# Adaptive scale and shift of the first two k tiles: half of the sum moved from VectorE to TensorE, with the weights as the stationary operand

## The chip, the cores and the metric

The kernel runs on one core of a Trainium2 chip. A core has a matrix engine (TensorE, PE in the rows), a vector engine (VectorE, DVE), a scalar engine (ScalarE, ACT), a general engine (GpSimd, POOL) and a queue that issues transfers (SyncE, SP). The metric is the time of one execution on the device in microseconds (us); several executions of a kernel are summed up by their median.

## What is computed

One layer of a streaming-encoder trunk on 512 tokens of width 2048. A conditioning vector c gives, by one matrix product, the scale, shift and gate of both sub-layers, and the modulated input goes into a token mixer and then an MLP:

```python
mod = c @ w_ada[l] + b_ada[l]
sh1, sc1, g1, sh2, sc2, g2 = [m[:, None, :] for m in jnp.split(mod, 6, axis=-1)]
h = x * (1.0 + sc1) + sh1
mix = token_mixer(h, w_in[l], ...)        # starts with proj = h @ w_in
x = layer_norm(ALPHA * x + g1 * mix, ln1_g[l], ln1_b[l])
h = x * (1.0 + sc2) + sh2
ff = jnp.square(jax.nn.relu(h @ w_ff1[l])) @ w_ff2[l]
x = layer_norm(ALPHA * x + g2 * ff, ln2_g[l], ln2_b[l])
```

Only the first line, for sc1 and sh1, and what waits for it at the very start, is touched by the change.

## The kernel before

Channels are cut into 16 **k tiles** of 128. No product with `w_in` over a k tile can begin before the scale and shift of that tile's 128 channels are known, so the kernel begins with `start_k(k, w)`, which prepares w tiles at once: first tile 0 alone, then tile 1 alone, then tiles 2 to 5, 6 to 9, 10 to 13, and 14 and 15.

`start_k` loads the columns of `w_ada` that belong to its tiles (256 columns for one tile, scale and shift, over 16 row blocks of 128) in pieces of 1 MB into the tile `raw`, of which there are four buffers. `ada_acc` (line 215) walks over the 16 row blocks on VectorE: each instruction multiplies one block by one column of c (`col("c", i)`, a value per partition) and adds it into `adaz`; the first is a multiply alone (line 67), the others multiply and add (line 63). For a single tile there are two sums, taken in turn (`ways=2`), so that an instruction doesn't depend on the one just ahead of it. What is left is the sum over the 128 partitions. That is done on TensorE (line 299): a 128x128 piece of `adaz` is the stationary operand and a column of ones the moving one, which gives one column of the bank `sc`. Such a matmul of full fp32 operands is carried out as two passes, each with its own weight load, so that 4 matmuls are 8 PE instructions in the trace.

Then follow on VectorE the bias (`mod`, line 301) and plus one (line 303), on ScalarE `hf` = x times scale plus shift (line 308), and `split` (line 120), which writes the high part of `hf` (ScalarE) and the low part (VectorE) into `acts`. Weights are split in the same way into `wh` (ScalarE) and `wl` (VectorE), the small ones of `wkw` into `kwh` and `kwl`. Every product is made of three matmuls, high by high, low by high, high by low: `mm3` (lines 196 to 198) with the weight stationary, `mm3n` (lines 208 to 210) with the activation stationary.

The loop over `KGROUPS` takes tiles 0 and 1 as its first group: for each of both tiles, 15 matmuls of `wA` and `wkw` (banks `sa`, `mm`, `sb`), then two blocks of `wqi` over both tiles (18 matmuls each, evacuated by ScalarE into `qi_n`), then two blocks of `wq` (24 each, evacuated into `q_t`). The order on each engine is set by a scheduler from the priorities in `PRIO`; each engine then runs its instructions strictly in that order. Transfers are all issued by SP, in order too, and an issue into a buffer waits until the buffer's last reader is done.

Of the kernel before, what the change touches and what calls it, by code (L numbers as in the profile page):

```python
# [51 lines left out]
def trunk_kernel(ctx, tc, A, out):  # L52
    nc = tc.nc
    V, S, G, T = nc.vector, nc.scalar, nc.gpsimd, nc.tensor

    def act(o, i, f=AF.Copy, **kw):
        S.activation(o, i, f, **kw)  # L57

    def tt(o, a, b, op):
        V.tensor_tensor(o, a, b, op=op)  # L60

    def stt(o, a, s, b, op0, op1):
        V.scalar_tensor_tensor(o, a, s, b, op0=op0, op1=op1)  # L63

    def ts(o, a, s1, s2, op0, op1=None):
        if op1 is None:
            V.tensor_scalar(o, a, s1, None, op0=op0)
        else:
            V.tensor_scalar(o, a, s1, s2, op0=op0, op1=op1)
# [11 lines left out]
    def prio(name):  # L81
        if name not in PRIO:
            name += str(stage_no[0])
        return tc.high_priority(offset=PRIO[name])

    def bank(n="mm"):
        if "two" in pools:
            return two_banks()[:, 0]
        return pools[n].tile([128, 512], F32, name=n)
# [9 lines left out]
    def col(n, i=0, w=1):  # L99
        o = COLS[n][0]  # L100
        return cols[:, o + i:o + i + w]
# [5 lines left out]
    ones = P.tile([128, 128], F32, name="ones")  # L107
# [12 lines left out]
    def split(h, l, src):  # L120
        act(h, src)
        tt(l, src, h.bitcast(F32), OP.subtract)

    def load(src, shape, pool=None, tag="raw", bufs=4, prio_="w_load"):
        r = (pool or rawp).tile(shape, F32, name=tag, bufs=bufs)
        with prio(prio_):
            nc.sync.dma_start(r, src)
        return r
# [86 lines left out]
    def ada_acc(srcs, n, brow=None, ways=1, pool=None):  # L215


        z = (pool or AZ[0]).tile([128, ways * n], F32, name="adaz", bufs=2 if pool else 1)
        if brow is not None:
            G.memset(z, 0.0)  # L220
            with prio("ada_bias"):
                nc.sync.dma_start(z[0:1, :], brow)
        i = 0
        for s in srcs:
            r = load(s, [128, s.shape[1], n], *ada_raw, prio_="ada_load")
            with prio("ada"):
                for j in range(s.shape[1]):
                    o = z[:, (i % ways) * n:(i % ways + 1) * n]
                    if i < ways and brow is None:
                        ts(o, r[:, j], col("c", i), None, OP.mult)  # L230
                    else:
                        stt(o, r[:, j], col("c", i), o, OP.mult, OP.add)
                    i += 1
            yield z
# [43 lines left out]
    FP = first.enter_context(tc.tile_pool(name="first", bufs=2, reuse_waits="tile"))  # L278
# [2 lines left out]

    def start_k(k, w):

        if w == 4:
            src = A["adaS4"][(k - 2) // 4]
        else:
            src = A["adaS2"][k // 14][:, :, 256 * (k % 2):256 * (k % 2 + w)]
        step = 8 // w
        ways = 2 if w == 1 else 1
        for i, z in enumerate(ada_acc([src[:, a:a + step] for a in range(0, 16, step)], 256 * w,  # L290
                                      ways=ways, pool=FP)):
            if i < 2 * w - 1:
                yield
        ps = bank("sc")
        mod = FP.tile([128, 2 * w], F32, name="mod")
        for j in range(2 * w):
            for a in range(ways):
                c0 = (a * 2 * w + j) * 128
                T.matmul(ps[:, j:j + 1], z[:, c0:c0 + 128], ones[:, 0:1], start=a == 0, stop=a == ways - 1)
        with prio("mod"):  # L300
            tt(mod, ps[:, 0:2 * w], col("bS", 2 * k, 2 * w), OP.add)
            sc_ = mod.rearrange("p (k two) -> p k two", two=2)[:, :, 0]
            ts(sc_, sc_, 1.0, None, OP.add)
            for j in range(w):
                xk = FP.tile([128, SEQ], F32, name="xk")
                nc.sync.dma_start(xk, A["xT"][k + j])
                hf = FP.tile([128, SEQ], F32, name="hf")
                act(hf, xk, AF.Identity, scale=mod[:, 2 * j:2 * j + 1], bias=mod[:, 2 * j + 1:2 * j + 2])
                split(acts[:, k + j, 0], acts[:, k + j, 1], hf)
        ready[0] = k + w  # L310
        yield

    def start_all():
        k = 0
        while k < KT:
            w = 1 if k < 2 else min(4, KT - k)
            yield from start_k(k, w)
            k += w
# [106 lines left out]
    with prio("index"):  # L425
# [19 lines left out]
        ps = bank("sa")  # L445
# [3 lines left out]
        for t in range(3):  # L449
# [10 lines left out]
            for hf in range(2):  # L460
                ps = bank("sa")
# [10 lines left out]
            for h in range(IH):  # L472
                ps = bank("sa")
                for i in range(2):
                    T.matmul(ps[:, 0:nk], qs[:, h // 2, h % 2], ks[:, i, 0:nk], start=i == 0, stop=i == 1)
                r = IX.tile([128, SEQ], F32, name="relu", bufs=2)
# [47 lines left out]
    def rms_rows(pool, acc, n_, b):  # L524

        ps = bank(b)
        for t in range(NT):
            T.matmul(ps[:, t:t + 1], acc[:, t * 128:(t + 1) * 128], ones[:, 0:1], start=True, stop=True)
        rs = pool.tile([128, NT], F32, name="st", bufs=4)
        act(rs, ps[:, 0:NT], AF.Sqrt, scale=1.0 / n_, bias=eps[:, 0:1])  # L530
        V.reciprocal(rs, rs)
        ps = bank(b)
        for t in range(NT):
            dg = pool.tile([128, 128], F32, name="dg", bufs=2)
            act(dg, ident, scale=rs[:, t:t + 1])
            T.matmul(ps[:, t * 128:(t + 1) * 128], ones, dg, start=True, stop=True)
        return ps

    def square_sum(pool, tiles, bufs=(2, 3)):
        acc = pool.tile([128, SEQ], F32, name="qh", bufs=bufs[0])  # L540
        act(acc, tiles[0], AF.Square)
        for y in tiles[1:]:
            sq = pool.tile([128, SEQ], F32, name="s", bufs=bufs[1])
            act(sq, y, AF.Square)
            tt(acc, acc, sq, OP.add)
        return acc
# [18 lines left out]
    def pv(i):  # L565
        return prm[:, i]
# [18 lines left out]
    with prio("ssm0"):  # L585
        lr, li = col("lr", 0, 16), col("li", 0, 16)
        dt, mag, ang, n, r, cs, sn, t0, t1, den, fr, fi, l4r, l4i = [pv(i) for i in range(14)]
# [64 lines left out]
        for j in range(1, 4):  # L652
            a = (hs[:, 0, :, j - 1:j], hs[:, 1, :, j - 1:j])
# [146 lines left out]
    with prio("glu"):  # L800
# [3 lines left out]
        for m in range(4):  # L804
            ps = bank("sb")
# [6 lines left out]
        ps = rms_rows(GL, square_sum(GL, [u_t[:, m] for m in range(4)], (1, 1)), 512, "sb")  # L812
# [121 lines left out]
    with prio("mixer"):  # L934
# [7 lines left out]
        ps = rms_rows(AT, square_sum(AT, [z_t[:, m] for m in range(4)]), 512, "sa")  # L942
# [76 lines left out]
    with prio("ln1"):  # L1019
        for t in range(NT):  # L1020
# [3 lines left out]
            for kq in range(4):  # L1024
                ps = bank(("sa", "sb")[kq % 2])
                for j in range(4):
                    k = 4 * kq + j
                    T.transpose(ps[:, j * 128:(j + 1) * 128], r1[:, t, k * 128:(k + 1) * 128], ident)
                hf = WO.tile([128, 4, 128], F32, name="hf2", bufs=3)
                for j in range(4):  # L1030
                    k = 4 * kq + j
# [46 lines left out]
    def ev_tile():  # L1078
        return ST.tile([128, 512], F32, name="ev", bufs=6)
# [52 lines left out]
    for i, j in QUARTERS:  # L1132
        r = ev_tile()
# [21 lines left out]
    with prio("tx"):  # L1155
        for c in range(2):
            kk = slice(4 * c, 4 * c + 4)

            def get(i, j):
                o = st_tile()  # L1160
                nc.sync.dma_start(o, hx_d[:, 8 * i + 4 * c:8 * i + 4 * c + 4, (lo_t, hi_t)[j]])
                return o
# [4 lines left out]
            a, b_ = get(0, 0), get(0, 1)  # L1167
# [236 lines left out]
    for e in range(NS):  # L1404
# [3 lines left out]
        if e == 0:  # L1408
# [3 lines left out]
            z = []  # L1412
# [91 lines left out]
    for t in range(NT):  # L1504
        for i in range(2):
            ps = bank()
# [102 lines left out]
```

## Time and profile before

| | us |
|---|---|
| median of 3 runs | 2272.72 |
| the runs | 2266.93 to 2273.12 |
| the profiled execution, its own time | 2262.95 |
| its span on the core | 2261.2 |
| PE busy | 2159.0 (95%) |
| DVE busy | 1873.2 (83%) |
| ACT busy | 1092.9 (48%) |

The profile lists the busy time of each engine, the span in slices, the chain of work that ended last, and the trace gives every instruction with its start, its duration and what its engine waited for. Durations of matmuls overlap, since they are pipelined: the time that one takes of a stream is the distance from its start to the start of the next.

### The profile page before, as it was taken

To read this page: it belongs to the slowest core of one execution; us is meant where nothing else is said; L and a number is where in the kernel's file an instruction comes from. 1 tells how busy PE (TensorE), PEld (TensorE's weight loads), DVE (VectorE), ACT (ScalarE), POOL (GpSimd) and SP (SyncE) were. 2 spreads that over 40 slices of the span, in tenths; PEclk is the share of its full clock that TensorE was granted. 3 is DMA by queue.
4 is the path that set the end of the run, shared out by engine and by line. 5 is a ranking of instruction groups with operands and counts; after the bars stand their busy time and mean duration, and the time that the engine had idled before them with its cause. 6 is when DMAs were issued, how large, how long until landed. Compare 5 with 4: busy or idle time off the path is not lost.

```text
span 2261.2 us, 30621 instructions
## 1 busy us (share of the span) xinstructions
PE 2159.0 (95%) x11947; PEld 1849.2 (82%) x11947; DVE 1873.2 (83%) x2520; ACT 1092.9 (48%) x1570; POOL 44.6 (2%) x55
## 2 busy tenths in 40 slices
PE   6999999988899999999999999999999999999997
PEld 4778887866676787899999999999888887878886
DVE  7886889998776776798778778778699989998788
ACT  3323434458855223666555555555444444444432
POOL 0000000000000000000000000000000000000000
PEclk9999999999999999999999999999999999999999
DMA  8877553264224576745654544553788988796562
GB/s 320 320 292 278 182 216 135 96 208 154 79 84 172 208 282 264 242 142 205 212 187 178 199 183 176 197 187 140 289 303 281 335 276 290 236 343 226 146 235 90
DMA packets 129626, 485.59 MB, mean 215 GB/s; under 512 B 15556, under 2 KB 38468, under 8 KB 88264
## 3 DMA queue, kind: packets, MB, share of 16 engines
q1 hardware_dynamic: 122952, 471.04, 56.9%
q0 software_dynamic: 6528, 12.58, 3.3%
q8 instruction: 94, 1.54, 0.3%
q14 instruction: 52, 0.43, 0.1%
HBM read 392.35 MB, written 78.64 MB: 208 GB/s over the span
## 4 chain that ended last, share of the span: by engine, by line
PE 44%; DVE 32%; DMA 15%; ACT 5%; issue 4%; DVEq 0%; SPq 0%; ACTq 0%
DMA raw<-in_wff_dram 11%; DVE wl L60 10%; PE two L1375 4%; PE two L1376 4%; PE two L1374 4%; DVE st L60 4%; PE mm L210 4%; PE mm L209 4%; PE mm L208 4%; PE mm L197 4%; PE mm L198 4%; PE mm L196 4%; DVE ffa L60 2%; DVE adaz L63 2%; DVE hc L60 2%
## 5 line engine op out<-in xcount | busy, mean ns | idle before, releaser
L57 ACT ACTIVATE wh<-raw 128x1024 fp32r<-128x1024 f32 x332 | 349.5, 1057 | 427.4 <-PE two L1376 137.9
L60 DVE TENSOR_TENSOR wl<-raw,wh 128x1024 fp32r<-128x1024 f32 x332 | 403.1, 1220 | 69.4 <-ACT wh L57 68.9
L1375 PE MATMUL two<-wl,hin 128*128 128x512 f32 x784 | 307.8, 393 | 3.3 <-DVE wl L60 3.0
L1374 PE MATMUL two<-wh,hin 128*128 128x512 f32 x784 | 307.1, 392 | 3.8 <-ACT wh L57 2.1
L1376 PE MATMUL two<-wh,hin 128*128 128x512 f32 x784 | 306.1, 390 | 0.0
L196 PE MATMUL mm<-acts,wh 128*128 128x512 f32 (+1 forms) x568 | 225.5, 400 | 7.3 <-ACT ve L57 3.8
L203 PE MATMUL mm<-acts,wl 128*128 128x256 f32 x720 | 209.4, 291 | 18.4 <-DVE wl L60 18.2
L197 PE MATMUL mm<-acts,wl 128*128 128x512 f32 (+1 forms) x568 | 223.6, 394 | 1.9 <-DVE wl L60 1.7
L198 PE MATMUL mm<-acts,wh 128*128 128x512 f32 (+1 forms) x568 | 223.6, 395 | 0.0
L63 DVE SCALAR_TENSOR_TENSOR adaz<-raw,cols,adaz 128x1024 f32<-128x1024 f32 (+2 forms) x180 | 198.3, 1112 | 17.5 <-DMA raw<-in_adaR_dram 13.4
L202 PE MATMUL mm<-acts,wh 128*128 128x256 f32 x720 | 206.1, 286 | 1.3 <-ACT ev L57 1.3
L204 PE MATMUL mm<-acts,wh 128*128 128x256 f32 x720 | 206.0, 286 | 0.0
L203 PE MATMUL mm<-tx,wl 128*128 128x256 f32 x720 | 203.8, 283 | 0.0
L204 PE MATMUL mm<-tx,wh 128*128 128x256 f32 x720 | 203.3, 282 | 0.0
L202 PE MATMUL mm<-tx,wh 128*128 128x256 f32 x720 | 201.9, 280 | 0.0
L1375 PEld LDWEIGHTS two<-wl,hin 128*128 128x128 f32 x784 | 147.6, 188 | 40.3 <-DVE wl L60 9.2
L1374 PEld LDWEIGHTS two<-wh,hin 128*128 128x128 f32 x784 | 147.5, 188 | 36.0 <-ACT wh L57 3.0
L209 PE MATMUL mm<-wl,acts 128*128 128x512 f32 x448 | 175.0, 391 | 1.2 <-DVE wl L60 1.0
L210 PE MATMUL mm<-wh,acts 128*128 128x512 f32 x448 | 174.7, 390 | 0.0
L208 PE MATMUL mm<-wh,acts 128*128 128x512 f32 x448 | 173.6, 391 | 0.2 <-DVE r L60 0.2
L1376 PEld LDWEIGHTS two<-wh,hin 128*128 128x128 f32 x784 | 147.6, 188 | 30.4
L203 PEld LDWEIGHTS mm<-acts,wl 128*128 128x128 f32 x720 | 140.6, 195 | 24.4 <-DVE wl L60 24.4
(316 smaller groups left out, 4539.1 us busy)
## 6 DMA issues: line engine op xcount, KB each, us to landing
raw<-in_wff_dram SPq DMA_DIRECT2D x128, 1024.0 KB, 6.4
hc_d<-hc SPq DMA_DIRECT2D x98, 512.0 KB, 3.8
hin<-hc_d SPq DMA_DIRECT2D x49, 1024.0 KB, 9.0
raw<-in_adaR_dram SPq DMA_DIRECT2D x48, 1024.0 KB, 5.1
raw<-in_adaS_dram SPq DMA_DIRECT2D x32, 1024.0 KB, 9.0
raw<-in_wo_dram SPq DMA_DIRECT2D x16, 1024.0 KB, 5.0
araw<-in_adaR_dram SPq DMA_DIRECT2D x16, 1024.0 KB, 6.3
raw<-in_wconv_dram SPq DMA_DIRECT2D x12, 1024.0 KB, 4.8
```

The costliest lines, as they stand in the source:

```text
L57: S.activation(o, i, f, **kw)
L60: V.tensor_tensor(o, a, b, op=op)
L196: T.matmul(ps, wh, xh, start=start, stop=False)
L197: T.matmul(ps, wl, xh, start=False, stop=False)
L198: T.matmul(ps, wh, xl, start=False, stop=stop)
L202: T.matmul(ps, wh, xh, start=start, stop=False, skip_group_check=True)
L203: T.matmul(ps, wl, xh, start=False, stop=False, skip_group_check=True)
L204: T.matmul(ps, wh, xl, start=False, stop=stop, skip_group_check=True)
L209: T.matmul(ps, xh, wl, start=False, stop=False)
L1374: T.matmul(ps[:, t], xh, h[:, k], start=first, stop=False, skip_group_check=True)
L1375: T.matmul(ps[:, t], xh, l[:, k], start=False, stop=False, skip_group_check=True)
L1376: T.matmul(ps[:, t], xl, h[:, k], start=False, stop=last, skip_group_check=True)
```

## The change

For tiles 0 and 1 alone (`w == 1`), VectorE sums only the first 8 of the 16 row blocks, in one sum instead of two. The other 8 blocks are not summed on VectorE at all: each 128x128 piece of the loaded weights is the stationary operand of a TensorE matmul and the column of c that belongs to it the moving one (16 matmuls, line 294 of the changed kernel), all accumulating into the bank `sc`. The two pieces of `adaz` are added to the same bank with the column of ones (2 matmuls, line 297). The tiles prepared four and two at a time are summed as they were.

```diff
-        step = 8 // w
-        ways = 2 if w == 1 else 1
-        for i, z in enumerate(ada_acc([src[:, a:a + step] for a in range(0, 16, step)], 256 * w,
-                                      ways=ways, pool=FP)):
-            if i < 2 * w - 1:
-                yield
         ps = bank("sc")
         mod = FP.tile([128, 2 * w], F32, name="mod")
-        for j in range(2 * w):
-            for a in range(ways):
-                c0 = (a * 2 * w + j) * 128
-                T.matmul(ps[:, j:j + 1], z[:, c0:c0 + 128], ones[:, 0:1], start=a == 0, stop=a == ways - 1)
+        if w == 1:
+
+            src = A["adaS2"][k // 14][:, :, 256 * (k % 2):256 * (k % 2 + 1)]
+            for z in ada_acc([src[:, 0:8]], 256, pool=FP):
+                yield
+            r = load(src[:, 8:16], [128, 8, 256], prio_="ada_load")
+            for i in range(8):
+                for j in range(2):
+                    T.matmul(ps[:, j:j + 1], r[:, i, 128 * j:128 * j + 128], col("c", 8 + i),
+                             start=(i, j) == (0, 0), stop=False, skip_group_check=True)
+            for j in range(2):
+                T.matmul(ps[:, j:j + 1], z[:, j * 128:(j + 1) * 128], ones[:, 0:1], start=False, stop=True,
+                         skip_group_check=True)
+        else:
...
+            for j in range(2 * w):
+                T.matmul(ps[:, j:j + 1], z[:, j * 128:(j + 1) * 128], ones[:, 0:1], start=True, stop=True)
```

The order of all engines changes within about the first 60 matmuls and is the same behind them; SP issues its transfers in the same order as before. Three places:

TensorE, from the last matmul of tile 0 (bank `sb`) to the first ones of tile 1 (bank `sa`); `sc` is the bank of the scale and shift. Before:

```order
L198 MATMUL sb<-acts,kwh 80x512
L299 MATMUL sc<-ones,adaz 128x1 x4
L208 MATMUL mm<-wh,acts 128x512 x2
L209 MATMUL mm<-wl,acts 128x512
L210 MATMUL mm<-wh,acts 128x512
L196 MATMUL sa<-acts,wh 128x512
```

In the changed kernel, the same place:

```order
L198 MATMUL sb<-acts,kwh 80x512
L294 MATMUL sc<-cols,raw 128x1 x16
L297 MATMUL sc<-ones,adaz 128x1 x2
L196 MATMUL sa<-acts,wh 128x512
L197 MATMUL sa<-acts,wl 128x512
```

Four matmuls on `adaz` became 16 on the raw weights and 2 on `adaz`, and the four matmuls of `wqi` that stood between them and tile 1 moved behind tile 1. For tile 0 it is the same 16 and 2, at the head of the engine's program.

ScalarE, from tile 1's preparation to the evacuations of the first `wqi` block; the rows `wh<-rw 128x1024` split the weights of the first and of the second `wqi` block. The difference:

```order
-L57 ACTIVATE wh<-rw 128x1024
 L57 ACTIVATE hf<-xk,mod 128x512
 L57 ACTIVATE acts<-hf 128x512
+L57 ACTIVATE wh<-rw 128x1024
 L57 ACTIVATE u_t<-mm 128x512 x2
-L57 ACTIVATE wh<-rw 128x1024
 L57 ACTIVATE qi_n_105<-mm 128x512
 L57 ACTIVATE qi_n_106<-mm 128x512
 L57 ACTIVATE qi_n_107<-mm 128x512
+L57 ACTIVATE wh<-rw 128x1024
```

The split for the first block moved behind tile 1's `hf`, and the split for the second block moved from ahead of the first block's three evacuations to behind them.

VectorE, the head of its program in the changed kernel; before, 16 rows of `adaz` and then `wl` and `kwl` stood ahead of `mod`:

```order
L67 TENSOR_SCALAR adaz<-raw,cols 128x256
L63 SCALAR_TENSOR_TENSOR adaz<-raw,cols,adaz 128x256 x7
L60 TENSOR_TENSOR mod<-sc,cols 128x2
L67 TENSOR_SCALAR mod<-mod 128x1
L60 TENSOR_TENSOR wl<-rw,wh 128x512
L60 TENSOR_TENSOR kwl<-rkw,kwh 128x80
L60 TENSOR_TENSOR acts<-hf,acts 128x512
```

Eight rows of `adaz` are gone, and `wl` and `kwl` of tile 0 moved behind `mod`, which waits for TensorE's bank `sc`.

## Rows read from the trace of the kernel before

**Rows 1.** Page, the chain that ended last: share of the span by engine.

```profile
PE 44%; DVE 32%; DMA 15%; ACT 5%; issue 4%; DVEq 0%; SPq 0%; ACTq 0%
```

**Rows 2.** Windows of 10 us: length, busy us, granted clock, DMA share, GB/s.

```profile
10.00:20.00 10.00, 5.24 (x16) 4.42 (x17) 9.09 (x25) 3.03 (x6) 0.00 (x0) 1.00 1.09 370
20.00:30.00 10.00, 8.54 (x40) 6.37 (x39) 8.55 (x15) 4.64 (x6) 0.00 (x0) 1.00 1.01 413
```

**Rows 3.** Chain of waits, 5 to 16 us: start, us, what.

```profile
7.43 5.24 DVE adaz L63 x13
...
12.81 1.85 PE sc L299 x8
```

**Rows 4.** VectorE's timeline around the second transfer's landing: start, us, instruction.

```profile
9.33 0.48 DVE L63 SCALAR_TENSOR_TENSOR adaz<-raw,cols,adaz 128x256 f32<-128x256 f32 x1
9.81 0.48 DVE L63 SCALAR_TENSOR_TENSOR adaz<-raw,cols,adaz 128x256 f32<-128x256 f32 x1
```

**Rows 5.** Line 299 in two windows: duration min/median/max ns, first and last start.

```profile
L299 PE MATMUL sc<-ones,adaz x8: 345/352/352, 12.8 to 14.3; 128*128 128x1 f32 x8
L299 PE MATMUL sc<-ones,adaz x16: 164/250/250, 53.2 to 54.8; 128*128 128x1 f32 x16
```

**Rows 6.** TensorE's timeline, tiles 0 and 1: start, us, instruction, idle before it.

```profile
16.60 0.79 PE L196 MATMUL sa<-acts,wh 128*128 128x512 f32 x1 [1.95 <-ACT acts L57]
...
18.90 0.63 PE L197 MATMUL mm<-acts,wl 128*128 128x512 f32 x1
19.33 0.60 PE L196 MATMUL mm<-acts,wh 128*128 128x512 f32 x1
19.75 0.41 PE L197 MATMUL mm<-acts,wl 128*128 128x512 f32 x1
...
21.38 0.39 PE L198 MATMUL sb<-acts,kwh 128*80 128x512 f32 x1
22.21 1.13 PE L299 MATMUL sc<-ones,adaz 128*128 128x1 f32 x8 [0.44 <-DVE adaz L63]
```

**Rows 7.** TensorE's timeline, a later place with single-column matmuls (line 254).

```profile
300.13 0.39 PE L475 MATMUL sa<-ks,qs 128*128 128x256 f32 x1 [0.53 <-ACT relu L57]
300.36 0.28 PE L254 MATMUL sc<-ones,adaz 128*128 128x1 f32 x2
...
303.28 0.63 PE L196 MATMUL mm<-acts,wh 128*128 128x512 f32 x1
303.71 0.63 PE L197 MATMUL mm<-acts,wl 128*128 128x512 f32 x1
```

**Rows 8.** Chain of waits, 24 to 62 us, around the first `wq` blocks.

```profile
36.15 0.24 PE mm L210
...
36.41 0.60 ACT qi_n L57
37.01 0.95 ACT wh L57
37.98 1.24 DVE wl L60
...
39.27 0.50 PE mm L197
...
46.98 0.74 PE mm L197
...
50.66 0.23 PE mm L196
```

**Rows 9.** SP's timeline; VectorE's first instruction on the next tiles' weights.

```profile
12.92 0.92 SPq L127 DMA_DIRECT2D raw<-in_adaS_dram  x2
...
25.88 0.75 DVE L67 TENSOR_SCALAR adaz<-raw,cols 128x1024 f32<-128x1024 f32 x1
```

**Rows 10.** Chain of waits, 140 to 160 us: a load of the third set of tiles.

```profile
148.05 0.33 SPq L306
...
148.47 7.68 DMA raw<-in_adaS_dram
```

More of the change, by code (lines that the diff above doesn't have):

```diff
@@ L282, in start_k @@
     def start_k(k, w):
[L284 to L287, printed above, removed]
-        step = 8 // w
-        ways = 2 if w == 1 else 1
-        for i, z in enumerate(ada_acc([src[:, a:a + step] for a in range(0, 16, step)], 256 * w,
-                                      ways=ways, pool=FP)):
-            if i < 2 * w - 1:
-                yield
         ps = bank("sc")
         mod = FP.tile([128, 2 * w], F32, name="mod")
-        for j in range(2 * w):
-            for a in range(ways):
-                c0 = (a * 2 * w + j) * 128
-                T.matmul(ps[:, j:j + 1], z[:, c0:c0 + 128], ones[:, 0:1], start=a == 0, stop=a == ways - 1)
+        if w == 1:
[11 more added lines that the diff above has]
+        else:
+            if w == 4:
+                src = A["adaS4"][(k - 2) // 4]
+            else:
+                src = A["adaS2"][k // 14][:, :, 256 * (k % 2):256 * (k % 2 + w)]
+            step = 8 // w
+            for i, z in enumerate(ada_acc([src[:, a:a + step] for a in range(0, 16, step)], 256 * w, pool=FP)):
+                if i < 2 * w - 1:
+                    yield
+            for j in range(2 * w):
+                T.matmul(ps[:, j:j + 1], z[:, j * 128:(j + 1) * 128], ones[:, 0:1], start=True, stop=True)
         with prio("mod"):
```

## Prediction

> **What bounds the kernel now.** I read the chain that ended last by engine first: TensorE 44%, VectorE 32%, transfers 15% [rows 1]. The reader is to see that no one engine sets the whole time; stages pass the end to each other, so a change is worth what it does in its own stage. The change touches the first 36 us only; from the end of the second `wqi` block on, the order of all engines is as before. There I read the windows [rows 2]: VectorE is busy 9.1 of 10 us and 8.6 of 10 us while TensorE is at 5.2 and 8.5, which makes VectorE look like the place to save. The chain of waits says what stands behind that [rows 3]: 13 sums on `adaz` (5.24 us, 0.403 us each), then the column sums on TensorE, 12.81 to 14.66 us, then `mod`, `hf`, the high part, and at 16.60 the first product [rows 6]. So for tile 0 the sums are on the path. What the trace doesn't say directly is when the second half of the weights lands: at 9.33 to 9.81 two sums are 0.48 us apart where the others keep 0.40 [rows 4], and 9.81 is the ninth sum, the first on the second transfer. I take 9.8 us as its landing.
>
> The price of a TensorE pass is in two rows [rows 5]: 8 passes start from 12.8 to 14.3 us, about 0.212 us apart; 16 passes from 53.2 to 54.8, 0.106 apart. That is the two levels of the clock: the 512-column products of tile 0 are 0.43 us apart up to 19.75 us (1.2 GHz) and 0.23 after it (2.4 GHz) [rows 6], although the window view prints a granted clock of 1.00 there [rows 2]; I go by the spacings.
>
> **Tile 0.** Removed: 8 of 16 sums on VectorE, 4 of 8 passes. Added: 16 matmuls, that is 32 passes, which need the second half, so they can't begin before 9.8 us. TensorE has done nothing until then and runs at its lower level. Before, from 9.8 to the end of the column sums: 14.66 - 9.8 = 4.9 us. After: 36 passes x 0.212 = 7.6 us. VectorE's eight sums now depend on each other; the seven behind the first start at 7.43 [rows 3], and even at twice 0.403 us they'd end by 7.4 + 5.6 = 13.0 us, while the 32 passes run to 16.6, so they are hidden and cost nothing, and what VectorE saves is worth nothing. **+2.8 us.** Bounds: at 0.106 all through, 3.8 us, -1.1; at the lower level only for the 3.1 us that tile 0's products needed (16.60 to 19.75, [rows 6]), 14.6 passes, then 21.4 x 0.106: 5.4 us, +0.5. `wl` and `kwl` of tile 0 now queue behind `mod` on VectorE; a `wl` of twice the size takes 1.24 us [rows 8], and ScalarE needs 1.95 us from the column sums to the first product [rows 6], so they are done by then. The low part is next on VectorE and, at half of 1.24 us, ready 0.6 us after the first product starts, before the third one needs it at 0.43 us each: no loss.
>
> **Tile 1.** Before, from the end of tile 0's column sums to the end of tile 1's: 23.34 - 14.66 = 8.7 us [rows 3, 6]; VectorE's sums ended it. After, TensorE ends it, since its passes stand behind tile 0's 15 products: 1.95 us + 5.0 us (16.60 to 21.6, the same start at the lower level) + 36 passes. Those start at the higher level. But a later place has such passes too [rows 7]: from 300.36 us on TensorE is given 16 of them between four products of 256 columns, and behind them the 512-column products go from 0.23 us apart to 0.43 at about 303. So I let the clock fall 2.7 us after they begin: 25 passes at 0.106, 11 at 0.212, 5.0 us. In all 12.0: **+3.3 us**. Bounds: all at the higher level, 3.8 us, +2.1; all at the lower, 7.6 us, +5.9.
>
> **Tile 1's products and the two `wqi` blocks.** Before, 23.34 to 36.39: 13.05 us, with a wait for `wl` in it. After: 1.95 us, then 15 + 18 products x 0.23 = 7.6 us without a wait. Then comes a new one: the second block's `wh` now stands behind the three evacuations on ScalarE, and its `wl` on VectorE behind that. The trace has the same pattern one block later [rows 8]: from the block's end at 36.39, 0.60 us of `qi_n`, 0.95 of `wh`, 1.24 of `wl`, first low product at 39.27, so 2.88 us, of which 3 products fill 0.7. Then 15 x 0.23 = 3.4 us. In all 15.85: +2.8 us. After the passes and 1.95 us of waiting I expect the lower level for 3.1 us again: 7 products x 0.2 = 1.4 us. **+4.2 us.** Bounds: +2.8 if the clock stays; one more fall across the new wait costs 8 x 0.2 = 1.6 us as from 46.98 to 50.66 [rows 8], so +5.8.
>
> **Transfers.** Two loads for tiles 2 to 5 now wait until TensorE, not VectorE, has read a buffer. The first pair was issued at 12.92 us and is first used at 25.88 [rows 9]; it would now be issued at about 17 and used some 8 us later than before, since tile 1 is later. Cost nothing; if that cover were gone, the 4 us of the issue. Queued behind them on SP are the loads of `wqi` and `wq`, used more than 20 us later.
>
> **Sum.** 2.8 + 3.3 + 4.2 = +10.3 us; with each part's bounds around the likeliest mechanism, 2.8 + 2.1 + 2.8 = 7.7 to 2.8 + 5.9 + 5.8 = 14.5. After that the shift is carried on: each stage starts from the one before. Against the profiled execution that is 2262.95 + 10.3 = 2273.3. That execution lies 9.8 us below the median of the runs shown, and a measurement gives a median: 2272.7 + 10.3 = 2283.0, own range 2280 to 2287.
>
> **Rivals.** (1) **The passes raise the clock like products do.** Then tile 0 costs +0.5; tile 1 is 1.95 + 15 x 0.23 + 0.2 for the low part + 3.8 = 9.4, +0.7; the rest +2.8: +4.0, 2276.7. For it: the engine is busy in both. Against it: the fall behind such passes [rows 7]. The Trainium skill, TensorE: Matmul & The Clock Gate, Part 1: The HAM clock gate, says that the lower level is the default and that activity releases it, whatever the number of matmuls; by that page the sum would be this rival's +4.0. The rows at 300 us lean against counting these passes so.
>
> (2) **The delay is taken up later.** At 148.47 the chain waits 7.68 us for a load of the third set of tiles [rows 10]. Had that load been issued in time whatever came ahead, it would swallow up to 7.7 us: 2275.3. Against it: the issue stands on SP behind line 306, which ends at 148.4 only because `hf` was late, so it shifts too.
>
> (3) **VectorE sets the pace**, not the path through TensorE, and the change pays: 16 sums x 0.403 = -6.4 us, 2266.3. For it: VectorE's 9.1 and 8.6 of 10 us [rows 2]. It decides from the point where 36 passes fit into the 4.9 us of tile 0, at 0.135 us a pass. Against it: 0.212 at that very place [rows 5].
>
> (4) **More falls of the clock** in later short waits, each 1.6 us [rows 8]; three beyond the sum give +15.1, 2287.8. For it: two waits of about 2 us follow one another now. Against it: the sum already has one fall, behind the passes, and the products of one burst warm the clock for the next.
>
> **Chances.** A measurement of this kernel tells about 0.3% (6.8 us) from no change. Forecast 0.58, nearly all of it slower by more than that; rival 1 0.18, rival 2 0.09, both within; rival 3 0.07, mostly within, since 6.4 is below the bound; rival 4 0.08. Slower: 0.54 + 0.08 = 0.62; same: 0.04 + 0.18 + 0.09 + 0.04 = 0.35; faster 0.03. The range goes down to rivals 1 and 2 and up to rival 4: 2275 to 2288; left out are rival 3 and the far ends.
>
> **What would show it.** Line 294 starts near 9.8 us with passes 0.21 apart, and the first 512-column product near 19.3 us instead of 16.6; tile 1's passes slow down part of the way; tile 1's products start 0.43 apart; TensorE idles about 2 us between the `wqi` blocks; line 299's successor for tiles 2 to 5 comes some 10 us later than 53.2. Wrong if: passes on raw weights are below 0.14 us at the start, the second transfer lands clearly before 9.8, or the shift at 55 us is gone by 160.

## The result and the profile after

The changed kernel takes 2282.61 us, median of six runs (2280.71 to 2283.45), against 2272.06 us for the kernel before on the same chip (six runs, 2266.93 to 2273.12). The ratio is 1.0051, 95% interval 1.0038 to 1.0064: slower by about 11 us. The profiled execution took 2282.96 us and has a span of 2281.2 us.

The page of the changed kernel, busy time by engine and the chain that ended last, answers to the table of before and to [rows 1]:

```profile
PE 2175.4 (95%) x12003; PEld 1864.1 (82%) x12003; DVE 1867.3 (82%) x2504; ACT 1093.2 (48%) x1570; POOL 44.6 (2%) x55
...
PE 40%; DVE 35%; DMA 16%; ACT 5%; issue 4%; DVEq 0%; SPq 0%; ACTq 0%
```

The page hardly shows the change: VectorE did 16 instructions and 6 us less, TensorE 56 more. The shares of the chain move by up to four points, but they also differ between two executions of the changed kernel (TensorE 40% and 42%, VectorE 35% and 32%), so little can be read from them. The windows of 10 us do show the change (columns as in [rows 2]):

```profile
10.00:20.00 10.00, 8.05 (x37) 7.96 (x38) 2.28 (x7) 2.63 (x5) 0.00 (x0) 1.00 1.09 368
...
30.00:40.00 10.00, 8.06 (x24) 6.30 (x25) 6.75 (x8) 3.58 (x5) 0.00 (x0) 0.58 0.64 224
```

The last of these windows in the kernel before:

```profile
30.00:40.00 10.00, 8.32 (x36) 6.26 (x35) 8.79 (x8) 4.54 (x8) 0.00 (x0) 1.00 1.03 413
```

Between 10 and 20 us VectorE is busy 2.3 us where it was 9.1 [rows 2], so the change relieved the engine that looked full, and TensorE is busy 8 us where it was 5.2. Between 30 and 40 us the granted clock is 0.58 where it was 1.00. TensorE's timeline of the changed kernel (start, us, engine, line, instruction, idle before it and what ended it) answers to [rows 6]:

```profile
9.90 6.96 PE L294 MATMUL sc<-cols,raw 128*128 128x1 f32 x32 [9.90 <-DMA raw<-in_adaS_dram]
16.72 0.99 PE L297 MATMUL sc<-ones,adaz 128*128 128x1 f32 x4
19.66 0.79 PE L196 MATMUL sa<-acts,wh 128*128 128x512 f32 x1 [1.95 <-ACT acts L57]
...
24.52 0.48 PE L198 MATMUL mm<-acts,wh 128*128 128x512 f32 x1
...
25.52 4.46 PE L294 MATMUL sc<-cols,raw 128*128 128x1 f32 x32
29.84 0.99 PE L297 MATMUL sc<-ones,adaz 128*128 128x1 f32 x4
32.77 0.79 PE L196 MATMUL sa<-acts,wh 128*128 128x512 f32 x1 [1.94 <-ACT acts L57]
...
38.06 0.53 PE L196 MATMUL sb<-acts,kwh 128*80 128x512 f32 x1
38.43 0.40 PE L197 MATMUL sb<-acts,kwl 128*80 128x512 f32 x1
...
38.90 0.40 PE L208 MATMUL mm<-wh,acts 128*128 128x512 f32 x1
...
44.81 0.98 PE L208 MATMUL mm<-wh,acts 128*128 128x512 f32 x3 [1.63 <-ACT wh L57]
...
51.39 1.20 PE L196 MATMUL mm<-acts,wh 128*128 128x512 f32 x4 [1.63 <-ACT wh L57]
```

The 32 passes on raw weights start with the second transfer and the four on `adaz` start at 16.72, so a pass takes (16.72 - 9.90) / 32 = 0.213 us. The column sums end at 17.71 instead of 14.66, the first product starts at 19.66 instead of 16.60 [rows 6]. Tile 1's passes stand behind the last product of tile 0 without a gap and take 5.3 us. Tile 1's products are 0.43 us apart up to 38.06. The first `wqi` block starts at 38.90, ahead of 44.81 there is the new wait between the two blocks, and the first `wq` product starts at 51.39.

What VectorE did, from its own timeline in the changed kernel:

```profile
7.26 3.61 DVE L63 SCALAR_TENSOR_TENSOR adaz<-raw,cols,adaz 128x256 f32<-128x256 f32 x7
17.75 0.16 DVE L60 TENSOR_TENSOR mod<-sc,cols 128x2 f32<-128x2 f32 x1 [6.88 <-PE sc L297]
...
30.86 0.16 DVE L60 TENSOR_TENSOR mod<-sc,cols 128x2 f32<-128x2 f32 x1 [5.87 <-PE sc L297]
...
34.84 0.75 DVE L67 TENSOR_SCALAR adaz<-raw,cols 128x1024 f32<-128x1024 f32 x1
```

Its share of the sum is done at 10.87 us. Then it sits idle for 6.88 us, and later for 5.87 us, until TensorE has the bank `sc`: before, TensorE waited for VectorE at these places [rows 3, 6].

### The profile page after: what moved, and what is told of

The parts are those of the page before. It is cut to its first block, busy times and chain, and to the rows that moved or that the text cites. A ratio compares the mean times of both kernels' runs of the same rounds, so it can differ in the third digit from the quotient of the medians.

```text
span 2281.2 us, 30717 instructions
## 1 busy us (share of the span) xinstructions
PE 2175.4 (95%) x12003; PEld 1864.1 (82%) x12003; DVE 1867.3 (82%) x2504; ACT 1093.2 (48%) x1570; POOL 44.6 (2%) x55
## 4 chain that ended last, share of the span: by engine, by line
PE 40%; DVE 35%; DMA 16%; ACT 5%; issue 4%; DVEq 0%; SPq 0%; ACTq 0%
DVE wl L60 11%; DMA raw<-in_wff_dram 10%; PE two L1385 4%; PE two L1386 4%; PE two L1384 4%; DVE st L60 4%; PE mm L197 3%; PE mm L198 3%; PE mm L196 3%; PE mm L210 3%; PE mm L209 3%; PE mm L208 3%; DVE ffa L60 3%; DVE adaz L63 2%; DVE hc L60 2%
## 5 line engine op out<-in xcount | busy, mean ns | idle before, releaser
L63 DVE SCALAR_TENSOR_TENSOR adaz<-raw,cols,adaz 128x1024 f32<-128x1024 f32 (+2 forms) x166 | 193.3, 1165 | 16.8 <-DMA raw<-in_adaR_dram 13.8
L203 PEld LDWEIGHTS mm<-acts,wl 128*128 128x128 f32 x720 | 139.2, 193 | 24.5 <-DVE wl L60 24.2
```

Source lines behind the costliest of these rows:

```text
L203: T.matmul(ps, wl, xh, start=False, stop=False, skip_group_check=True)
```

## The experiments

All are read at the same four places: the end of tile 0's and of tile 1's column sums, the first product of the first `wq` block, and the first column sum of the third set of four tiles, each as its distance from the first profile of the kernel before (14.66, 23.34, 38.01 and 143.75 us), beside the ratio of the times to the kernel before on the same chip. The last column is the interval minus one, times 2271 us. The distances come from one execution each, and the two of the change lie 1.9 us apart at the first `wq`, so differences of that size between rows tell little.

| kernel | tile 0 | tile 1 | first `wq` | third set | ratio [95%] | in us |
|---|---|---|---|---|---|---|
| before, again | 0.0 | 0.0 | 0.0 | +0.2 | 1.0007 [0.9985, 1.0029] | -3 to +7 |
| the change | +3.1 | +7.5 | +13.4 | +13.6 | 1.0051 [1.0038, 1.0064] | +9 to +15 |
| the change, again | +2.9 | +5.5 | +11.5 | +11.9 | 1.0044 [1.0028, 1.0060] | +6 to +14 |
| tile 0 only | +2.8 | +4.5 | +7.1 | +7.2 | 1.0027 [1.0009, 1.0045] | +2 to +10 |
| tile 1 only | -0.1 | +4.3 | +10.1 | +10.0 | 1.0057 [1.0035, 1.0079] | +8 to +18 |
| fillers ahead | +1.6 | +3.8 | +9.7 | +10.0 | 1.0067 [1.0047, 1.0087] | +11 to +20 |
| split ahead | +2.8 | +7.3 | +10.4 | +9.9 | 1.0034 [1.0021, 1.0047] | +5 to +11 |
| a quarter on TensorE | -0.2 | +1.6 | +1.7 | +0.8 | 1.0003 [0.9988, 1.0019] | -3 to +4 |
| before, filled | +0.4 | +1.0 | +2.8 | +2.9 | 1.0013 [0.9990, 1.0036] | -2 to +8 |

**The kernel before, again.** No edit. The first profile of the kernel before was 9 us below its median, and the profile of the changed kernel lies 20 us above it, twice what the medians differ by. The question was which part of that belongs to the change.

> The kernel before, once more, for a second profile. In the two profiles so far the changed kernel is 13.4 us late at the end of the second wqi block (49.77 against 36.39 us) and 12.4 us late at 70 us, and stays so up to 300 us; between 300 and 710 us it falls back by 7.5 us more, to 20 in span, while the medians differ by 10.5. Theory (the loss is made in the first 60 us, the 7.5 us are where the clock of TensorE happens to fall in an execution): this profile ends the second wqi block at 36.4 us again, within 0.5 us, is within 1 us of the first profile up to 300 us, and then falls behind it by 5 to 10 us, to a time near 2272. Rival (the later 7.5 us belong to the change): it stays within 2 us of the first profile to the end, near 2263.

It follows the first profile within about 0.2 us up to the third set and within 0.8 us at line 254 (first start 299.62 against 300.36 [rows 7]), and ends 8.6 us later (span 2269.8 against 2261.2). The window from 300 to 710 us of the first profile of the kernel before, and under it of this second one (columns as in [rows 2]; the granted clock is the third number from the end):

```profile
300.00:710.00 410.00, 377.32 (x1727) 289.61 (x1728) 349.78 (x852) 239.87 (x516) 11.90 (x19) 0.98 0.41 144
```

```profile
300.00:710.00 410.00, 376.49 (x1706) 291.08 (x1705) 343.88 (x844) 236.82 (x509) 11.91 (x19) 0.95 0.41 143
```

The same program had a granted clock of 0.98 there once and 0.95 once, and between the first pass of line 254 at 300 us and its last one ahead of 700 us (661.0 and 665.7) the second execution falls behind by 5.4 us. So the clock behind 300 us differs from one execution to the next whatever the change, and the first profile was a lucky one. From 300 us on the profiles can't be set against each other one by one; up to 300 us they can.

**The change for tile 0 only.** Tile 1 is summed as before, in two sums on VectorE.

```diff
-        if w == 1:
+        if w == 1 and k == 0:
...
+        elif w == 1:
+            src = A["adaS2"][k // 14][:, :, 256 * (k % 2):256 * (k % 2 + 1)]
+            for i, z in enumerate(ada_acc([src[:, a:a + 8] for a in range(0, 16, 8)], 256, ways=2, pool=FP)):
+                if i < 1:
+                    yield
...
```

> The change for tile 0 alone; tile 1 is summed on VectorE as before. Theory (the passes run at the lower level of the clock on the path, and tile 1's part and the moved order cost apart from it): column sums of tile 0 end at 17.7 us against 14.66, +3.1; second wqi block ends at 39.5 to 41 us against 36.39 of before and 49.77 of the changed kernel; no new wait between the wqi blocks, since the order of ScalarE there is that of before; time 3 to 4 us above before, near 2275.5. Rival (the loss is made in the later part, or by the buffers that come free later): as late as the changed kernel, 2282.

Tile 0 costs what it costs in the changed kernel, +2.8 us. But 7.1 us were lost at the first `wq` block, about twice what was expected. TensorE's timeline of this kernel behind tile 0's products:

```profile
26.67 1.13 PE L307 MATMUL sc<-ones,adaz 128*128 128x1 f32 x8 [1.00 <-DVE adaz L63]
...
29.98 0.63 PE L196 MATMUL sa<-acts,wh 128*128 128x512 f32 x1
30.41 0.63 PE L197 MATMUL sa<-acts,wl 128*128 128x512 f32 x1
```

Tile 1's sums, now started later on VectorE, end later (+4.5 us), and tile 1's products come at the lower level, 0.43 us apart, where before they stood 0.23 apart (25.51 to 28.72 us). So here the delay at the head is followed by a second loss, in the clock.

**The change for tile 1 only**, by the same edit with `k == 1`.

> The change for tile 1 alone; tile 0 is summed on VectorE as before. Theory: column sums of tile 0 end at 14.7 us; tile 1's passes begin at 21.6, where its products end, and end at 25.5 to 27.1 against 23.34; tile 1's products run at the lower level for at least 3 us; 2.2 us of TensorE idle between the wqi blocks, since ScalarE's order there is that of the changed kernel; second wqi block ends at 43 to 46 us; time 6.5 to 9 us above before, 2278.5 to 2281. Rival (tile 0 alone makes the loss and the rest follows from it): less than 2 us above before.

Ten us at the first `wq` block, more than was expected. Its timeline on TensorE:

```profile
21.95 4.87 PE L294 MATMUL sc<-cols,raw 128*128 128x1 f32 x32
26.68 0.99 PE L297 MATMUL sc<-ones,adaz 128*128 128x1 f32 x4
30.26 0.80 PE L196 MATMUL sa<-acts,wh 128*128 128x512 f32 x1 [2.59 <-ACT acts L57]
...
41.56 0.98 PE L208 MATMUL mm<-wh,acts 128*128 128x512 f32 x3 [1.63 <-ACT wh L57]
```

Although tile 0 is done as before, 36 passes take 5.7 us here; all at the higher level would be 36 x 0.106 = 3.8 [rows 5]. The wait between the `wqi` blocks is the same as in the whole change, so it belongs to the order that comes with tile 1. The parts don't add up (7.1 + 10.1 against 13.4). Tile 1's own steps in the table are those of the whole change (4.4 and 5.8 us here, 4.4 and 5.9 there); what is too much is what tile 0 alone loses behind its sums, 1.7 us at tile 1's sums on VectorE and 2.6 us at its products, and in the whole change tile 1's passes stand in that place.

**Fillers ahead.** The changed kernel with 22 matmuls of ones by ones (128 columns, two passes each) at the head of TensorE's program, while it has nothing to do.

```diff
+    warm = bank("sc")
+    with tc.high_priority(offset=60000):
+        for _ in range(22):
+            T.matmul(warm[:, 0:128], ones, ones, start=True, stop=True)
```

> The changed kernel with 22 matmuls of 128 columns on a tile of ones ahead of tile 0's passes, while TensorE would idle; their result is not used. Theory (the passes cost 0.212 us because the clock is at its lower level, and such passes don't raise it themselves): passes of tile 0 go 0.106 us apart, or change to 0.212 part of the way; column sums end at 13.8 to 15.5 us against 17.7; second wqi block 2 to 6 us earlier than in the changed kernel; time 2277 to 2281. Rival (the pass on freshly landed weights costs 0.21 us for another reason than the clock, such as reading them): spacing stays at 0.21 and the time at 2282.

TensorE's timeline:

```profile
1.14 6.55 PE L112 MATMUL sc<-ones 128*128 128x128 f32 x44 [1.14 <-POOL ones L108]
9.61 5.80 PE L298 MATMUL sc<-cols,raw 128*128 128x1 f32 x32 [1.92 <-DMA raw<-in_adaS_dram]
15.27 0.99 PE L301 MATMUL sc<-ones,adaz 128*128 128x1 f32 x4
...
23.10 3.63 PE L298 MATMUL sc<-cols,raw 128*128 128x1 f32 x32
```

The passes of tile 0 take 5.66 us instead of 6.82, between the 3.4 us of the higher and the 6.8 of the lower level, and those of tile 1 the 3.5 us of the higher. So the price of a pass is a matter of the clock, as the prediction had it, and tile 0's sums end 1.4 us earlier than in the changed kernel. At the first `wq` block 3.7 us are saved against the first profile of the change, but only 1.8 against its second one (the change, again), where tile 1's passes ran at the higher level without fillers. The time didn't follow: 1.0067, not below the changed kernel. The early shift of 10.0 us lies just outside the interval of 11 to 20 us. What the rest is, these runs don't tell.

**The change, again**, on another chip.

> The changed kernel once more, on one chip with the next three. Theory (the loss is made in the first 60 us): first product of the second group of tiles at 70.0 us again, within 0.5, against 57.6 of before; behind that the two kernels' profiles differ only where the clock of TensorE falls; time 9 to 14 us above before. Rival (the loss also grows later): the distance to before's profiles grows with every stage.

It is slower by the same amount within the intervals. Early on it is 1.9 us ahead of the first profile of the change, where the expectation allowed 0.5: tile 0's products left the lower level sooner and took 5.2 us instead of 5.9, and tile 1's 32 raw passes took 3.5 us, all at the higher level, where the first profile has 4.3. So how long the lower level lasts, and where the clock falls in these passes, changes from execution to execution too.

**Split ahead.** The changed kernel with a higher priority for the load of the second `wqi` block. With it the scheduler puts that block's split on ScalarE ahead of the first block's three evacuations, as it was before the change.

```diff
-PRIO = dict(cols=40000, ...
+PRIO = dict(w_first=4020, cols=40000, ...
...
-            for k, h, l in w_ks(A["wqi"][b], k0, k1, pace, FP):
+            for k, h, l in w_ks(A["wqi"][b], k0, k1, pace, FP, prio_="w_first" if gi == 0 and b == 1 else "w_load"):
```

> The changed kernel, with one load moved: the weights of the second wqi block are loaded ahead of the next tiles' weights, and with that ScalarE splits them ahead of the first block's evacuations, as in the kernel before. Theory (the wait of 2.0 us between the wqi blocks comes from that order): the wait is gone, the second block starts right behind the first, the first wq product comes 2.0 to 2.6 us earlier than in the changed kernel (48.8 to 49.4 against 51.39); the column sums stay at 17.7 and 30.8. Rival (the block would have waited for something else, such as the load): the first wq product stays at 51.4.

TensorE goes through both blocks without a wait; its timeline at the start of the first and around the end of the second:

```profile
38.41 0.40 PE L208 MATMUL mm<-wh,acts 128*128 128x512 f32 x1
...
46.37 0.39 PE L210 MATMUL mm<-wh,acts 128*128 128x512 f32 x1
48.38 0.73 PE L196 MATMUL mm<-acts,wh 128*128 128x512 f32 x2 [1.63 <-ACT wh L57]
```

From the first `wqi` product to the first `wq` product it takes 48.38 - 38.41 = 10.0 us, in the changed kernel 51.39 - 38.90 = 12.5. So the wait costs 2.5 us. In the time that is 1.0034 against 1.0044 on the same chip: in the right direction, but within the intervals.

**A quarter on TensorE.** VectorE sums 12 row blocks, TensorE takes the last 4: 16 passes instead of 32.

```diff
-            for z in ada_acc([src[:, 0:8]], 256, pool=FP):
-                yield
-            r = load(src[:, 8:16], [128, 8, 256], prio_="ada_load")
-            for i in range(8):
+            for i, z in enumerate(ada_acc([src[:, 0:8], src[:, 8:12]], 256, pool=FP)):
+                if i < 1:
+                    yield
+            r = load(src[:, 12:16], [128, 4, 256], prio_="ada_load")
+            for i in range(4):
```

> TensorE takes 4 of the 16 row blocks instead of 8, VectorE 12; so 16 passes and 4 instead of 32 and 4. Theory (the price is passes times 0.212 us behind the second transfer, for tile 0): passes end at 9.8 + 16 x 0.212 = 13.2, VectorE's twelve sums, 0.52 us apart, at 13.0, column sums end at 14.1 us, 0.6 ahead of before and 3.6 ahead of the changed kernel; the order on ScalarE is that of before, so no wait between the wqi blocks; first wq product at 38 to 41 us; time within 4 us of before. Rival (the price is fixed, for having passes on raw weights at all): column sums end near 17 us, time near the changed kernel's.

TensorE's timeline, and under it VectorE's behind the column sums:

```profile
10.08 3.54 PE L295 MATMUL sc<-cols,raw 128*128 128x1 f32 x16 [10.08 <-DMA raw<-in_adaS_dram]
13.48 0.99 PE L298 MATMUL sc<-ones,adaz 128*128 128x1 f32 x4
17.07 0.79 PE L196 MATMUL sa<-acts,wh 128*128 128x512 f32 x1 [2.59 <-ACT acts L57]
```

```profile
14.51 0.16 DVE L60 TENSOR_TENSOR mod<-sc,cols 128x2 f32<-128x2 f32 x1 [1.37 <-PE sc L298]
14.59 0.69 DVE L60 TENSOR_TENSOR wl<-rw,wh 128x512 fp32r<-128x512 f32 x1
15.20 0.23 DVE L60 TENSOR_TENSOR kwl<-rkw,kwh 128x80 fp32r<-128x80 f32 x1
15.35 0.15 DVE L67 TENSOR_SCALAR mod<-mod 128x1 f32<-128x1 f32 x1
```

Twenty passes instead of 36 end at 14.47, 0.2 us ahead of the kernel before: moving the work shows no fixed price, it costs by the pass. The gain is lost at once, since the plus one (the second `mod`) stands behind `wl` and `kwl` on VectorE, which makes the step to the first product 2.59 us instead of 1.95. The order of the `wqi` blocks is that of before, so the wait between them is not there. The time is that of the kernel before.

**The kernel before, filled.** The opposite test: the kernel before with TensorE kept at work, by 46 filler matmuls at its head and 8 (16 passes) between tile 0's column sums and its first product.

```diff
+        for _ in range(46):
+            T.matmul(warm[:, 0:128], ones, ones, start=True, stop=True)
...
+        if k == 0:
+            for _ in range(8):
+                T.matmul(ps[:, 128:256], ones, z[:, 0:128], start=True, stop=True)
```

> The kernel before with 46 matmuls of 128 columns on ones ahead of tile 0's column sums and 8 more between these and the first product, where TensorE idles; their results are not used. Theory (the start runs at the lower level only because TensorE had nothing to do): column sums of tile 0 take 0.95 us instead of 1.85, end at 13.7 instead of 14.66; tile 0's products start at 15.6 and go 0.23 us apart from the first; first product of the second group of tiles 1 to 3 us earlier than 57.6; time 1 to 3 us below before, which the comparison can hardly tell. Rival: the fillers end late and push the path: later than before.

TensorE's timeline:

```profile
1.13 12.78 PE L112 MATMUL sc<-ones 128*128 128x128 f32 x92 [1.13 <-POOL ones L108]
13.97 1.05 PE L303 MATMUL sc<-ones,adaz 128*128 128x1 f32 x8
15.28 2.05 PE L308 MATMUL sc<-adaz,ones 128*128 128x128 f32 x16 [0.25 <-DVE mod L60]
...
17.40 0.39 PE L201 MATMUL sa<-acts,wl 128*128 128x512 f32 x1
17.63 0.40 PE L200 MATMUL sa<-acts,wh 128*128 128x512 f32 x1
...
22.59 1.73 PE L303 MATMUL sc<-ones,adaz 128*128 128x1 f32 x8 [1.80 <-DVE adaz L63]
...
26.51 0.63 PE L214 MATMUL mm<-wh,acts 128*128 128x512 f32 x1
26.93 0.63 PE L200 MATMUL sa<-acts,wh 128*128 128x512 f32 x1
```

With fillers ahead and between, the eight column passes take 1.05 us instead of 1.85 [rows 3], and tile 0's products are 0.23 us apart from the second on: with TensorE at work ahead of it, the head runs at the higher level. But the expected gain of 1 to 3 us didn't come; the rival did, and the first `wq` product is 2.8 us late. The fillers ran until 13.9 us and held up tile 0's column sums, and with them VectorE. TensorE started tile 0's last product 1.0 us sooner than before (20.40 against 21.38, [rows 6]) and then waited 1.80 us for VectorE's sums of tile 1, so what the higher level saved there was worth nothing. Behind that wait the products are 0.43 us apart again (26.51, 26.93). No kernel of this study is faster than the one before.

## Why the prediction was right, and where its terms were off

The forecast was 2283.0, the median came to 2282.6, and slower by more than 0.3% held. Its mechanism stands. In the first profile of the change all three terms came out larger, two of them by more than 1 us.

**Tile 0.** +2.8 was predicted, +3.1 measured. The second transfer lands where it was put (passes start at 9.90), a pass costs 0.213 us where 0.212 was taken from [rows 5], and VectorE's dependent sums are done 6.9 us before TensorE has the bank. The clock didn't rise in the 36 passes: the last four, from 16.72, are still 0.21 us apart.

**Tile 1.** +3.3 predicted, +4.4 measured (from one end of column sums to the other 30.83 - 17.71 = 13.12 us against 8.7 before; 12.0 was predicted). Tile 0's products took 5.86 us instead of 5.0, because they stayed at the lower level until 24.5 us, and the passes 5.3 instead of 5.0. In the second profile of the change the same term is 28.79 - 17.60 - 8.7 = +2.5, since no pass was slow there and tile 0's products took 5.2 us. So +3.3 lies between two executions, and its bounds, +2.1 to +5.9, held both.

**Tile 1's products and the `wqi` blocks.** +4.2 predicted, +5.9 measured (30.83 to 49.77 = 18.94 us against 13.05), and about as much in the second profile: from the column sums to the first `wq` product it is 49.52 - 28.79 = 20.7 us against 14.7. The new wait came as priced. The chain of waits of the changed kernel, which answers to [rows 8]:

```profile
42.95 0.24 PE mm L210
43.21 0.60 ACT qi_n L57
43.81 0.95 ACT wh L57
44.79 1.24 DVE wl L60
46.07 0.50 PE mm L209
```

From the end of the first block at 43.19 to the first low product at 46.07 it is 2.88 us, to the hundredth what the pattern one block later had given; the kernel with the split ahead was 2.5 us faster there. **The step that was mis-sized is the lower level behind the passes**: 7 products at 0.2 us extra were counted, for as long as tile 0's products had needed before (16.60 to 19.75, [rows 6]). In the changed kernel it lasted from 32.77 to 38.43, 13 products, which is 1.2 of the 1.7 us. One place was taken as the measure of how long the lower level lasts; it lasted 3.2 us there, 4.9 us for tile 0 in the changed kernel and 5.7 us for tile 1, and 3.6 and 6.1 us in its second profile. What sets its length stays open.

**Transfers.** Nothing was predicted, and they are not the cause. SP in the changed kernel, which answers to [rows 9]:

```profile
16.89 0.80 SPq L127 DMA_DIRECT2D raw<-in_adaS_dram  x2
```

They are issued at 16.89, 4 us later as foreseen, and first used at 34.84, 9 us later: the cover held.

**The sum and the rest of the way.** The terms add to +13.4 at the first `wq` block where +10.3 was predicted. One us comes back at once, since the kernel before had a fall of the clock from 46.98 to 50.66 [rows 8] that the changed one doesn't have: line 309, for tiles 2 to 5, starts at 65.62 instead of 53.25, +12.4. Behind it the lower level lasts longer once more (70.07 to 75.78 us, before 57.62 to 60.76), which takes that us again: +13.6 at the third set. After that the shift is carried on, as the prediction said, with +12.8 at line 254 (313.13 against 300.36); in the second profile it is +11.9 and +11.0. To the end the medians differ by 10.6 us. In the table, the shift at the third set lies within the interval of the time, 6 to 10 us wide, in seven of the eight rows below the first and just below it in the eighth. So the time is the early shift, within what a measurement tells. That the total met the forecast by 0.4 us, though the early terms were 1 to 3 us larger, is luck of that size; whether the difference is given back behind 300 us or is the uncertainty of the medians stays open.

**The rivals.** Rival 1, that the passes raise the clock as products do, falls: TensorE ran 36 passes back to back from 9.90 to 17.71 us, the last ones were as far apart as the first, and the products behind them and 1.95 us of waiting began 0.43 us apart. The Trainium skill's rule that was set beside it (TensorE: Matmul & The Clock Gate, Part 1: The HAM clock gate) is not borne out by these passes at that place. Rival 2, that a later load swallows the delay, falls too. The load of [rows 10] is for tiles 14 and 15 and not for the third set, whose column sums stand ahead of it. What stands behind it are the column sums of tiles 14 and 15, before and in the changed kernel:

```profile
170.03 0.95 PE L299 MATMUL sc<-ones,adaz 128*128 128x1 f32 x8
```

```profile
182.46 0.95 PE L309 MATMUL sc<-ones,adaz 128*128 128x1 f32 x8
```

They come 12.4 us later, so of the 13.6 us ahead of that load no more than 1.2 are taken up, and not 7.7.

Rival 3, that VectorE sets the pace, falls by VectorE's own rows: it waits 6.88 and 5.87 us for `sc`. A pass cost 0.213 us, above the 0.135 from which this rival would decide; 36 passes didn't fit into 4.9 us, and in the quarter on TensorE 20 passes did, with column sums that end 0.2 us ahead of before. Rival 4, more falls of the clock, is half right: there were more products at the lower level than counted, all in the bursts behind column sums, up to 76 us. From 80 to 310 us the granted clock is 1.00 in both profiles of the change.

**Against which time.** The sum was made against the profiled execution and set on the median, which was 9.8 us higher. The second profile of the kernel before shows that this was right: the same program ended 8.6 us later with the same first 300 us. Set on the profiled execution, the forecast would have been 2273.3 and wrong.

## What to carry to other kernels

Before work is moved from a busy engine to an idle one, ask in which of its states the idle one will do it: at the head of a kernel TensorE ran at its lower level, and 36 small passes cost 7.8 us where the same stretch had taken 4.9 with VectorE's sums. When two engines share work, choose the shares by when each would end, not by halves of the data: the halves cost 12 to 13 us early on, the quarter under 2, though it gained nothing either. Price the order too: 2.5 us of the early loss came from a split that the scheduler had moved behind three evacuations, and no line of the change speaks of it. And a level of the clock that lasted 3 us at one place need not last 3 us at the next: here it was 3 to 6.

## What was not expected of the hardware

Single-column passes left TensorE at its lower level although the engine was busy with them without a gap for 7.8 us, while 12.8 us of 128-column passes ahead of the same place had it at the higher one (the kernel before, filled). Passes that began at the higher level slowed part of the way in some executions: 32 of them took 4.3 us at 25.52 in the changed kernel and 5.7 us at 9.61 behind the fillers, between the 3.4 and 6.8 us of the two levels. In its second profile 32 such passes at 24.72 took 3.5 us and didn't slow.

The granted clock between 300 and 710 us differed from 0.95 to 0.98 in two executions of one program, and the spans by 8.6 us, 0.4%: as much as the effect in question.

Two sums on VectorE, taken in turn, start 0.40 us apart [rows 3]; one sum, where each instruction needs the one ahead of it, has seven in 3.61 us, 0.52 us apart. Here that was hidden.
